# Odd tokens' rows by block transposes, their mean square by column sums, and three low parts by DMA, in a one-core decoder trunk

## The chip, the core and the metric

The kernel runs on one core of one Trainium2 chip. The metric is the device time of one execution in microseconds (us), the median of several runs. The engines are named as the profile names them: PE is TensorE's matrix multiplier (PEld its weight loads), DVE is VectorE, ACT is ScalarE, POOL is GpSimd, which here only issues accumulating DMAs, and SP is SyncE, which issues the other DMAs. Each of them runs its own instructions in order and waits on semaphores for the others.

## What is computed

One layer of a decoder trunk on x of 1024 tokens by 1024 channels, in fp32: a mixing block, then an MLP. The change lies where the first residual ends and the MLP begins:

```python
m = jax.nn.sigmoid(sa) * y_a + jax.nn.sigmoid(sb) * y_b
x = x + jnp.einsum("bsd,de->bse", m, w_o[l])          # called x1 here

h = rms_norm(x, g_mlp[l])                              # x / sqrt(mean(x*x) + EPS) * g
f = jnp.square(jax.nn.relu(jnp.einsum("bsd,df->bsf", h, w_1[l])))
x = x + jnp.einsum("bsf,fd->bsd", f, w_2[l])
return rms_norm(x, g_final)
```

## The kernel before

Activations lie with channels on the 128 partitions and tokens along the free axis. The tokens are held as even and odd ones: `x1[kk, o, c2]` is a tile of 128 x 1024 with o = 0 for even and o = 1 for odd tokens; its two halves are two blocks of 128 channels, kk and c2 say which. x1 thus has four tiles for each kind of token (x1000, x1001, x1100, x1101 and x1010, x1011, x1110, x1111 in the profile's full names, which the shown rows cut to `x`).

The three large products (w_a_out "a", w_o "o", w_1 "u") each run as seven block products of half size (p = 1 to 7, in the order 1, 2, 6, 7, 4, 5, 3) for four pairs of row blocks i. Every operand is split in a high part, rounded to the matmul's format, and a low part, the rest; a block product is 4 x 3 = 12 matmuls of 512 columns: high x high, high x low, low x high. The right operand's parts are `g{w}{p}h` and `g{w}{p}l` (halves 0 and 1 by c2), the left one's `o{i}_{p}` or `g{w}{i}_{p}` (both parts in one tile).

A low part is made in one of two ways. `low`: ACT copies the high part, DVE subtracts it from the source. `split_dma` (L61 to L67): ACT writes minus the rounded source (L65), POOL issues a DMA that adds the source to it (L66), ACT copies the high part (L67); DVE isn't used. Today the second operand of "u" (p = 2) and most left operands go the second way.

The stretch in question is written out by hand: `gseq` lists the block products in order, n counts them, and `GX[n]` names what else is recorded in step n; a small planner (`clk`, `at`, `dve`, `later`, `vector_work`, `flush`) decides where DVE's instructions stand among each other. Steps o0 = 28 to u0 = 56 are the products with w_o; from u0 the first eight products with w_1 follow (p = 1 for i = 0 to 3: banks gu0a to gu3a, then p = 2 on the same banks). Behind them the loop over `useq` continues with p = 6, 5, 7, 3, 4 for i = 0 and 1 (banks f0b, f1b, f0c, f1c, f0d, f1d, f0c, f1c, f0d, f1d), then the other row blocks.

For the even tokens (`x1_sq`, `x1_add`, `x1_turn`, `x1_cols`, `x1_root`, `x1_diag`, `x1_spread`, `x1_normed`): ACT squares the eight halves, DVE adds the squares to one tile, four matmuls with a column of ones sum it over the channels (`cs`, 128 tokens on partitions each), DVE and ACT form the root and its reciprocal (`stm`), diagonal matrices of it (`rdm`) times ones spread it over all partitions (`rbm`), and DVE normalises x1 in place. `x1_turn` transposes x1 in blocks of 32 x 32 on DVE (a row kk, th is one tile `x1r`) and SP writes them to DRAM; `x_block` reads them back in the second matrix stage (`d`), eight DMAs a block, as the residual's rows. The odd tokens have another way: `x1_rows` (step u0) transposes their x1 with 32 PE instructions into PSUM (`tr`), ACT squares and sums each row from there, DVE copies the rows out, SP writes them, and `x_block` reads a block with one DMA.

The left operands of "u" with p = 5, 6, 7, 3 for i = 0, 1 are sums of blocks of w_1: `up_lhs` makes s1, s2, s4, s3 (tiles `s`, five buffers in turn, so that the sixth, s4_1, takes s1_0's) on DVE and splits them by `split_dma` to o0_6, o1_6, o0_5, o1_5, o0_7 and so on.

Of the kernel before, what the change touches and what calls it, by code (L numbers as in the profile page):

```python
# [9 lines left out]
F32 = mybir.dt.float32  # L10
F32R = mybir.dt.float32r
I32 = mybir.dt.int32
AF = mybir.ActivationFunctionType
ALU = mybir.AluOpType

P = 128
S = 1024
# [13 lines left out]
def trunk_kernel(ctx: ExitStack, tc: tile.TileContext, x, xt_in, xt_eo, vecs, w_in, w_a_out, w_b_out,  # L31
# [1176 lines left out]
    def g_parts(w, p, c2):  # L1208
# [3 lines left out]
        if w == "u" and p == 2:  # L1212
            split_dma(src, h, l)
            at("A", 2.0)
            return
# [3 lines left out]
    def g_t(w, c2, *ns):  # L1219
# [4 lines left out]
        b11, b12, b21, b22 = (r[kk, o, c2] for kk in range(2) for o in range(2))  # L1224
# [41 lines left out]
    def g_mm(w, i, p):  # L1266
# [4 lines left out]
        for k in range(4):  # L1271
            h, l = (a[w, p, k // 2][:, HALVES[k % 2]] for a in (gh, gl))
# [97 lines left out]
    x1d = dp.tile([4, P, D], F32, name="x1d")  # L1370
    x1t = dp.tile([2, 2, P, S], F32, name="x1t")


    sqs = []

    def x1_sq(i, m_):
        s = EV(f"sq{i}{m_}")
        nc.scalar.activation(s, x1[i // 2, 0, i % 2][:, HALVES[m_]], AF.Square)
        sqs.append((at("A", 0.62, clk["V"]), s))

    def x1_add(n=1):
        for _ in range(n):
            ready, s = sqs.pop(1)
            later(ready, 0.63, tt, sqs[0][1], sqs[0][1], s, ALU.add)

    def x1_turn(kk):
        for th in range(2):
            r = T(f"x1r{kk}{th}")
            for c2 in range(2):
                src = x1[kk, 0, c2].rearrange("p (m h b j) -> p h m b j", m=2, h=2, j=32)[:, th]  # L1390
# [3 lines left out]
            nc.sync.dma_start(x1t[kk, th], r)  # L1394

    def x1_cols():

        sqs.append(bank("cs"))
        for n in range(4):
            nc.tensor.matmul(sqs[1][:, n:n + 1], sqs[0][1][:, n * P:(n + 1) * P], ones[:, 0:1],  # L1400
                             start=True, stop=True)
        at("P", 0.9)

    def x1_rows(*ts):
        for t in ts:
            o, n = divmod(t, 4)
            if n == 0:
                rst[o] = cp.tile([P, 6, 4], F32, tag="st6", name=f"stm{o}", bufs=2)
            rows = T(f"x1r{t}")
            for kk in range(2):  # L1410
                ps = bank(f"tr{t}{kk}")
                for c in range(4):
                    nc.tensor.transpose(ps[:, c * P:(c + 1) * P],
                                        x1[kk, o, c // 2][:, c % 2 * HS + n * P:c % 2 * HS + (n + 1) * P],
                                        ident)
                at("P", 0.45)
                if (t, kk) == (4, 0):
                    unread = T("sq")
                a = unread[:, HALVES[kk]]
                nc.scalar.activation(a, ps, AF.Square, accum_out=rst[o][:, kk, n:n + 1])  # L1420
                at("A", 0.63, clk["P"])

                def copy(rows, kk, ps, t):
                    nc.vector.tensor_copy(
                        rows[:, HALVES[kk]].rearrange("p (g c j) -> p c g j", g=4, c=4),
                        ps.rearrange("p (c g j) -> p c g j", g=4, c=4))
                    if kk:
                        nc.sync.dma_start(x1d[t - 4], rows)

                later(clk["P"], 0.63, copy, rows, kk, ps, t)  # L1430
            if t == 7:
                x1_root(1)
            if o:
                vector_work(clk["V"])

    def x1_root(o):

        if o == 0:
            rst[o] = cp.tile([P, 6, 4], F32, tag="st6", name=f"stm{o}", bufs=2)
        a, b, v, s = (rst[o][:, i, :] for i in range(4))  # L1440
        if o:
            tt(v, a, b, ALU.add)
# [666 lines left out]
```

## Time and profile before

| | |
|---|---|
| median of 3 runs | 1544.25 us (1544.06 to 1544.28) |
| the profiled execution | 1544.42 us |
| its span, first to last instruction | 1542.6 us |
| granted TensorE clock | 0.999 |
| instructions | 19197 |

The profile is of one execution. Its page gives the busy time of each engine and the chain of work that ended last; a timeline lists instructions in order of time, start and length in us, with neighbours of one kind merged (x32 is 32 of them, the length then from the first's start to the last's end), and in brackets the idle time before one and what ended it. Matmuls overlap: a single one is listed with 0.39 us, but starts follow each other every 0.23. In the rows of one line, a group has its count, then the shortest, median and longest duration in ns and the first and last start; a DMA's time to landing is counted from the start of its issue. A row of windows has the window, its length, and then each engine's busy time and instructions (PE, PEld, DVE, ACT, POOL), the clock, the DMA share and GB/s.

### The profile page before, as it was taken

The numbers are of one execution on the slowest core, as the hardware profiler recorded it, in microseconds if no ns is written. First come the engines' busy times: TensorE is split into PE (matmuls) and PEld (weight loads), VectorE is DVE, ScalarE is ACT, GpSimd is POOL, SyncE is SP. The second block draws the span as 40 slices with busy tenths as digits, with TensorE's granted clock in tenths as the row PEclk, the third lists the DMA queues.
The fourth block names the chain that finished last, engine by engine and source line by source line (L and its number), as shares of the span: only waits on it lengthen the run. The fifth ranks groups of instructions, "written<-read, shape, count | busy, mean of one in ns | idle before, by whom it ended". The sixth has DMA issues, their size and how long they took to land.

```text
span 1542.6 us, 19197 instructions
## 1 busy us (share of the span) xinstructions
PE 1533.0 (99%) x6782; PEld 1260.9 (82%) x6782; DVE 1222.4 (79%) x1648; ACT 903.7 (59%) x1261; POOL 184.4 (12%) x219
## 2 busy tenths in 40 slices
PE   9999999999999999999999999999999999999998
PEld 7888788888888888888888888888888888888886
DVE  6899999978999997478579889755555558888897
ACT  6648576567567667445275777554444475555553
POOL 0000000002222222000022332000000001111110
PEclk9999999999999999999999999999999999999999
DMA  8776978898997889953579897333333779998862
GB/s 347 195 192 159 251 189 218 220 273 212 254 253 196 194 194 240 316 174 111 181 204 297 200 219 180 137 123 112 112 114 112 240 217 231 223 224 220 209 130 110
DMA packets 132032, 307.82 MB, mean 200 GB/s; under 512 B 13488, under 2 KB 35504, under 8 KB 131936
## 3 DMA queue, kind: packets, MB, share of 16 engines
q1 hardware_dynamic: 101488, 230.60, 46.0%
q0 software_dynamic: 30304, 75.74, 26.9%
q8 instruction: 53, 0.87, 0.2%
q14 instruction: 43, 0.35, 0.1%
q10 hardware_dynamic: 144, 0.26, 0.0%
HBM read 147.69 MB, written 58.72 MB: 134 GB/s over the span
## 4 chain that ended last, share of the span: by engine, by line
PE 93%; DMA 2%; issue 2%; DVE 1%; ACT 0%; POOL 0%; SPq 0%; POOLq 0%; DVEq 0%
PE z L726 18%; PE d L1866 15%; PE yb L1097 8%; PE e L1993 3%; PE keep L1866 2%; PE z L258 1%; PE rg L534 1%; PE rg L536 1%; PE rg L535 1%; DMA x<-in_x_dram 1%; DMA zo<-zs 1%; DVE x L462 0%; DMA o<-s 0%; DMA xc<-in_xt_dram 0%; PE f1d L1552 0%
## 5 line engine op out<-in xcount | busy, mean ns | idle before, releaser
L726 PE MATMUL z<-xh,win_h 128*128 128x512 f32 x400 | 124.9, 390 | 0.0
L726 PE MATMUL z<-xl,win_h 128*128 128x512 f32 x400 | 124.5, 389 | 0.0
L1878 DVE TENSOR_TENSOR acc<-acc,d 128x1024 f32<-128x1024 f32 x72 | 87.8, 1219 | 33.3 <-PE d L1866 32.7
L726 PE MATMUL z<-xh,win_l 128*128 128x512 f32 x400 | 98.2, 391 | 0.0
L726 PEld LDWEIGHTS z<-xh,win_l 128*128 128x128 f32 x400 | 75.1, 188 | 16.9
L726 PEld LDWEIGHTS z<-xh,win_h 128*128 128x128 f32 x400 | 75.0, 188 | 16.7 <-ACT win_h L67 0.7
L637 DVE SCALAR_TENSOR_TENSOR y<-u,vec,y 128x511 f32<-128x511 f32 (+14 forms) x120 | 88.2, 735 | 0.0
L726 PEld LDWEIGHTS z<-xl,win_h 128*128 128x128 f32 x400 | 75.1, 188 | 15.8
L542 ACT ACTIVATE g<-rg,vec 96x1024 f32<-96x1024 f32 x32 | 35.6, 1112 | 85.0 <-issue 43.2
L637 DVE SCALAR_TENSOR_TENSOR yt<-u,vec,yt 128x511 f32<-128x511 f32 (+6 forms) x112 | 82.4, 736 | 0.0
L637 DVE SCALAR_TENSOR_TENSOR y<-yt,csum,y 128x511 f32<-128x511 f32 (+6 forms) x112 | 82.4, 736 | 0.0
L66 POOL DMA_DIRECT2D win_l<-win_raw x25 | 21.8, 871 | 324.6 <-ACT win_l L65 313.4
L1540 ACT ACTIVATE o<-s 128x512 fp32r<-128x512 f32 x56 | 33.7, 623 | 45.7 <-DVE s L1524 26.4
L66 POOL DMA_DIRECT2D zo<-zw x42 | 36.6, 872 | 130.4 <-ACT zo L65 113.5
L486 DVE SCALAR_TENSOR_TENSOR v<-xb,vec,v 128x1023 f32<-128x1023 f32 (+2 forms) x36 | 46.2, 1282 | 7.1 <-ACT v L477 6.3
L1097 PE MATMUL yb<-hgh,wb_h 128*128 128x512 f32 x168 | 51.7, 389 | 0.0
L1097 PE MATMUL yb<-hgl,wb_h 128*128 128x512 f32 x168 | 51.7, 389 | 0.0
L66 POOL DMA_DIRECT2D db_1l<-wr x7 | 6.1, 870 | 309.5 <-ACT db_1l L65 286.9
L1097 PE MATMUL yb<-hgh,wb_l 128*128 128x512 f32 x168 | 41.0, 389 | 0.0
L1063 DVE TENSOR_TENSOR o<-s,o 128x512 fp32r<-128x512 f32 x56 | 37.3, 683 | 1.4 <-ACT o L1540 1.4
L65 ACT ACTIVATE zo<-zw 128x512 fp32r<-128x512 f32 x42 | 26.2, 625 | 20.1 <-PE z10f L914 2.1
L1097 PEld LDWEIGHTS yb<-hgh,wb_h 128*128 128x128 f32 x168 | 31.5, 188 | 6.6
(1805 smaller groups left out, 4667.0 us busy)
## 6 DMA issues: line engine op xcount, KB each, us to landing
w_raw<-in_w_dram SPq DMA_DIRECT2D x34, 512.0 KB, 5.6
fr<-fd SPq DMA_DIRECT2D x32, 512.0 KB, 6.2
wr<-in_w_dram SPq DMA_DIRECT2D x32, 512.0 KB, 6.5
zw<-in_w_in_dram SPq DMA_DIRECT2D x28, 512.0 KB, 6.3
win_raw<-in_w_in_dram SPq DMA_DIRECT2D x25, 512.0 KB, 6.8
win_l<-win_raw POOLq DMA_DIRECT2D x25, 512.0 KB, 6.9
zo<-zw POOLq DMA_DIRECT2D x42, 256.0 KB, 5.7
gates<-zg SPq DMA_DIRECT2D x32, 256.0 KB, 3.8
```

Source lines behind the costliest of these rows:

```text
L65: nc.scalar.activation(l, src, AF.Copy, scale=-1.0)
L66: nc.gpsimd.dma_start(l, src, accum_op=ALU.add)
L486: nc.vector.scalar_tensor_tensor(v[:, d:S], a[:, 0:S - d], cbw_c[:, w * 12 + t:w * 12 + t + 1], v[:, d:S], ALU.mult, ALU.add)
L542: nc.scalar.activation(a, gps.pop((n, gi))[:HD, :], AF.Sigmoid, bias=(ba_c, bx_c)[gi][:, n:n + 1])
L637: nc.vector.scalar_tensor_tensor(o[:, k:], a[:, 0:HS - k], c, o[:, k:], ALU.mult, add)
L726: nc.tensor.matmul(zps[s][:, HALVES[hf]], w[:, k, :], xw[k][part][hf], start=n == 0, stop=n == 23)
L1063: tt(l, src, h.bitcast(F32), ALU.subtract)
L1097: nc.tensor.matmul(ps[hf], a, b[:, HALVES[hf]], start=n == 0, stop=n == len(todo) - 1)
L1540: nc.scalar.activation(o[:, 0], src, AF.Copy)
L1866: nc.tensor.matmul(o, a, b, start=n == 0 and (p != 1 or g == 0), stop=n == len(todo) - 1, skip_group_check=p == 1 and g > 0)
L1878: tt(acc[p, q2], acc[p, q2], ps, ALU.add)
L1993: nc.tensor.matmul(o, a, b, start=n == 0 and t not in LOADED, stop=n == len(todo) - 1, skip_group_check=t in LOADED)
```

## The change

The odd tokens take the even tokens' way. Their eight halves are squared on ACT between steps 23 and u0 (in another order, halves of p = 5 first), added on DVE, and summed over channels by four matmuls that stand in front of gu1a (`G_MID`); root and diagonals follow in step u0 + 1, and the spread in front of gu2a (before it stood in front of gu3a). `x1_turn` takes the token kind and a list of row halves: the odd tokens' first two tiles are transposed on DVE ahead of the last additions to x1 and the squares (step 27), the other two between the normalising of x1010, x1011 and that of x1110, x1111 (step u0 + 2). All of `x1_rows` is gone: 32 PE transposes, eight squares from PSUM, eight copies. `x_block` reads odd rows like even ones, with eight DMAs a block.

The low parts of the right operand p = 5 of "u" (gu5l0, gu5l1) and half of p = 1 (gu1l1) are made by `split_dma`. The left sums s1, s2 of w_1 and the operands made of them (o0_6 and others) are recorded one step later, and the parts of p = 5 and 6 in another order.

```diff
-        if w == "u" and p == 2:
+        if w == "u" and (p in (2, 5) or (p, c2) == (1, 1)):
             split_dma(src, h, l)
...
         for k in range(4):
+            if k == 0 and (w, p, i) in G_MID:
+                f, *a = G_MID[w, p, i]
+                f(*a)
...
-    x1d = dp.tile([4, P, D], F32, name="x1d")
-    x1t = dp.tile([2, 2, P, S], F32, name="x1t")
+    x1d = dp.tile([2, 2, 2, P, S], F32, name="x1d")
...
+    def x1_sq(o, i, m_):
+        n = len(sqt)
+        if o == 0 or 0 < n < 5:
+            s = EV(f"sq{o}{i}{m_}")
+        else:
+
+            if n in (0, 6):
+                x1_sq.t = T(f"sqs{n}")
+            s = x1_sq.t[:, HALVES[0 if n in (0, 6) else 1]]
+        if o:
+            sqt.append(s)
+        nc.scalar.activation(s, x1[i // 2, o, i % 2][:, HALVES[m_]], AF.Square)
+        sqs[o].append((at("A", 0.62, clk["V"]), s))
...
-    def x1_turn(kk):
-        for th in range(2):
-            r = T(f"x1r{kk}{th}")
+    def x1_turn(o, kk, *ths):
+        for th in ths:
+            r = T(f"x1r{o}{kk}{th}")
...
-    def x1_cols():
+    def x1_cols(o):
 
-        sqs.append(bank("cs"))
+        sqs[o].append(bank(f"cs{o}"))
         for n in range(4):
-            nc.tensor.matmul(sqs[1][:, n:n + 1], sqs[0][1][:, n * P:(n + 1) * P], ones[:, 0:1],
+            nc.tensor.matmul(sqs[o][1][:, n:n + 1], sqs[o][0][1][:, n * P:(n + 1) * P], ones[:, 0:1],
                              start=True, stop=True)
...
-    def x1_rows(*ts):
...
+    G_MID = {("u", 1, 1): (x1_cols, 1), ("u", 1, 2): (x1_spread, 1)}
...
-        23: ((x1_normed, 0, 0),), 24: ((g_parts, "u", 1, 0), (g_parts, "u", 1, 1)),
-        25: ((x1_normed, 1, 0),), 26: ((g_parts, "u", 2, 0),), 27: ((g_parts, "u", 2, 1),)}.items()})
+        23: ((x1_normed, 0, 0), (x1_sq, 1, 0, 1), (x1_sq, 1, 1, 1)), 24: ((g_parts, "u", 1, 0), (g_parts, "u", 1, 1), (x1_sq, 1, 2, 1)),
+        25: ((x1_normed, 1, 0), (x1_add, 1), (x1_sq, 1, 3, 1)),
+        26: ((g_parts, "u", 2, 0), (x1_add, 1, 2), (x1_sq, 1, 0, 0)),
+        27: ((g_parts, "u", 2, 1), (x1_add, 1), (x1_sq, 1, 1, 0), (x1_sq, 1, 2, 0), (x1_turn, 1, 0, 0, 1))}.items()})
     u0 = 2 * o0
     GX.update({u0 + n: v for n, v in {
-        0: ((g_lhs, "u", 1, 2), (up_lhs, 0, 6), (x1_rows, 4, 5, 6, 7)),
-        1: ((x1_diag, 1),), 2: ((x1_spread, 1), (up_lhs, 1, 6)),
-        3: ((x1_normed, 0, 1), (x1_normed, 1, 1), (g_t, "u", 0, 1), (g_t, "u", 1, 1)),
-        4: ((g_t, "u", 0, 2), (g_t, "u", 1, 2)), 5: ((g_parts, "u", 6, 0),),
-        6: ((g_parts, "u", 6, 1), (g_parts, "u", 5, 0), (up_lhs, 0, 5)),
-        7: ((g_parts, "u", 5, 1), (up_lhs, 1, 5), (g_t, "u", 0, 3), (g_t, "u", 1, 3))}.items()})
+        0: ((g_lhs, "u", 1, 2), (x1_add, 1, 2), (flush,), (x1_add, 1), (flush,)),
+        1: ((x1_root, 1), (x1_diag, 1), (up_lhs, 0, 6)),
+        2: ((x1_normed, 0, 1), (g_t, "u", 0, 1), (flush,), (up_lhs, 1, 6), (x1_turn, 1, 1, 0, 1),
+            (x1_normed, 1, 1)),
+        3: ((g_parts, "u", 5, 0), (g_t, "u", 0, 2), (flush,), (g_t, "u", 1, 1)),
+        4: ((g_t, "u", 1, 2), (g_parts, "u", 6, 0)),
+        5: ((g_parts, "u", 6, 1), (g_parts, "u", 5, 1)), 6: ((up_lhs, 0, 5),),
+        7: ((up_lhs, 1, 5), (g_t, "u", 0, 3), (g_t, "u", 1, 3))}.items()})
...
+            if n == u0:
+                x1_sq(1, 3, 0)
             g_get(n, g_mm)
...
     def x_block(b, q2):
         a = T(f"xb{b[0]}{b[1]}_{q2}")
-        if b[0]:
-            nc.sync.dma_start(a.rearrange("p (q c) -> p q c", q=2),
-                              x1d[2 * q2:2 * q2 + 2, :, b[1] * HS:(b[1] + 1) * HS].rearrange("q p c -> p q c"))
-            return a
-
-        src = x1t[b[1], q2].rearrange("(g i) (q b x) -> q b i g x", g=4, q=2, b=4)
+
+        src = x1d[b[0], b[1], q2].rearrange("(g i) (q b x) -> q b i g x", g=4, q=2, b=4)
```

72 lines of the change are left out of this document (19 added, 53 removed).

## The prediction

> **What bounds the kernel now.** I read the page first: busy time, then the chain of work that ended last.
>
> ```profile
> span 1542.6 us, 19197 instructions
> ...
> PE 1533.0 (99%) x6782; PEld 1260.9 (82%) x6782; DVE 1222.4 (79%) x1648; ACT 903.7 (59%) x1261; POOL 184.4 (12%) x219
> ...
> PE 93%; DMA 2%; issue 2%; DVE 1%; ACT 0%; POOL 0%; SPq 0%; POOLq 0%; DVEq 0%
> ```
>
> TensorE is busy 99% of the span and makes 93% of the chain. The change can gain only what it takes out of TensorE's own stream or out of its few waits there, and it loses whatever wait it puts in. Next I read TensorE's timeline around the odd tokens' rows (columns: start, length, engine, line, what, count).
>
> ```profile
> 897.40 0.95 PE L1400 MATMUL cs<-ones,sq 128*128 128x1 f32 x8
> 898.21 0.49 PE L1274 MATMUL go2e<-go5h,go 128*128 128x512 f32 x1
> ...
> 901.32 1.16 PE L1465 MATMUL rbm<-rdm,ones 128*128 128x128 f32 x8
> 902.24 0.48 PE L1274 MATMUL go3e<-go5h,go 128*128 128x512 f32 x1
> ...
> 918.66 3.65 PE L1413 MATMUL tr<-ident,x 128*128 128x128 f32 x32
> 922.07 0.48 PE L1274 MATMUL gu1a<-gu1h,gu 128*128 128x512 f32 x1
> ```
>
> ```profile
> 947.57 0.39 PE L1552 MATMUL f0c<-gu5h,o 128*128 128x512 f32 x1
> ...
> 953.01 0.39 PE L1552 MATMUL f0d<-gu7h,o 128*128 128x512 f32 x1
> ...
> 953.86 0.73 PE L1552 MATMUL f0d<-gu7h,o 128*128 128x512 f32 x2 [0.24 <-DMA o<-s]
> ...
> 959.20 0.39 PE L1552 MATMUL f0c<-gu3h,o 128*128 128x512 f32 x1
> ```
>
> Twelve matmuls make a product. From 947.57 to 953.01 two of them take 5.44 us without a wait, 2.72 each, 0.227 per matmul. The next two, to 959.20, take 6.19: there 0.75 us is lost today, as left low parts (o0_7, then o1_7) land late: the row at 953.86 names such a DMA as what ended its wait. From 959.20 on both kernels run the same instructions on TensorE, so how much earlier or later that matmul starts is the result.
>
> **Part 1, TensorE's own work.** Removed: 32 transposes, 918.66 to 922.07, 3.41 us. Added: four column sums, as the even tokens have them, 897.40 to 898.21, 0.81. What the step back to 512-wide matmuls costs stands behind either block and cancels. **Gain 2.60** if nothing waits.
>
> **Part 2, the wait that the column sums bring.** They stand behind gu0a, at 918.66, and need all eight odd squares added up. What VectorE does before that, from its rows:
>
> ```profile
> 887.32 1.48 DVE L462 TENSOR_TENSOR sq<-sq,sq 128x512 f32<-128x512 f32 x2
> ...
> 893.37 2.49 DVE L462 STREAM_TRANSPOSE x1r<-x 128x512 f32<-128x512 f32 x4
> 895.77 0.65 DVE L462 TENSOR_TENSOR x<-xe,go0e 128x512 f32<-128x512 f32 x1
> ...
> 899.34 0.13 DVE L1443 TENSOR_SCALAR stm<-cs 128x4 f32<-128x4 f32 x1
> ...
> 908.13 0.68 DVE L462 TENSOR_TENSOR x<-xe,go0e 128x512 f32<-128x512 f32 x1
> 908.73 2.72 DVE L462 SCALAR_TENSOR_TENSOR x<-x,vec,rbm 128x512 f32<-128x512 f32 x4
> 911.36 0.68 DVE L462 TENSOR_TENSOR x<-xe,go1e 128x512 f32<-128x512 f32 x1
> ...
> 936.40 2.36 DVE L462 TENSOR_TENSOR gt2u<-x,x 128x1024 f32<-128x1024 f32 x2
> 938.67 0.69 DVE L1528 TENSOR_TENSOR s<-w_raw,w_raw 128x512 f32<-128x512 f32 x1
> ...
> 946.54 0.68 DVE L1526 TENSOR_TENSOR s<-w_raw,s 128x512 f32<-128x512 f32 x1
> ...
> 953.00 1.22 DVE L1063 TENSOR_TENSOR gu7l<-x,gu7h 128x1024 fp32r<-128x1024 f32 x1
> ```
>
> Start to start an add takes 0.60 (908.13 to 908.73), one that needs the add before it about 0.71 (1.48 for two), four normalising steps 2.63 (908.73 to 911.36), four block transposes 2.40 (893.37 to 895.77), a 1024-wide subtraction 1.14 (936.40 to 938.67 is two). Normalising ends at 911.36 as before (gu1l1, gone to a DMA, may let it end 0.1 or 0.2 sooner). Then: a square add 0.60, an x1 add 0.60, two chained square adds 1.31, an x1 add 0.60: 914.5. Four block transposes, to 916.9; a square add 0.60; the last x1 add 0.60, to 918.1; three chained square adds 2.13: 920.2, with the head start 920.1. TensorE stands from 918.66 to 920.1, 1.45 us, and its weights then load uncovered: 0.92 for four small matmuls after a wait (901.32 to 902.24) against 0.81 in the stream (the sums at 897.40), 0.11 more. Behind the waiting sums stand gu1a and all that follows. Of the 2.60, **1.04 is left**. What is late is the last x1 add, as transposes run ahead of it. Bounds: no wait (2.60 kept) to 0.5 us more of it, should ScalarE's last square start one 512-wide step late.
>
> The four spread matmuls come one product earlier. Even tokens needed 1.98 from the variance (899.34) to the spread (901.32); here the sums end at 921.0 and their variance is read by 921.1, so 923.1, and gu1a (2.72) covers to 923.7. Without that cover TensorE would stand those 2 us.
>
> **Part 3, the fifth right operand.** Its parts cost VectorE 2 x 1.14 less and ScalarE 2 x 0.95 more, and ScalarE's order changes:
>
> ```profile
> 938.63 0.58 ACT L1331 ACTIVATE f<-gu1a 128x512 f32<-128x512 f32 x1
> ...
> 939.78 1.05 ACT L1216 ACTIVATE gu6h<-gt2u 128x1024 fp32r<-128x1024 f32 x1
> 940.73 1.04 ACT L1216 ACTIVATE gu5h<-x 128x1024 fp32r<-128x1024 f32 x1
> 941.68 0.62 ACT L65 ACTIVATE o<-s 128x512 fp32r<-128x512 f32 x1
> ```
>
> VectorE after the change: spread done 924.7, four normalising steps 2.63, one subtraction 1.14, two left sums 1.31 (the second needs the first), four transposes 2.40, four normalising steps 2.63, three 1024-wide and one 512-wide step 4.02: gt2u1 ends at about 939.0. Before it ended at 936.40 + 2.36 = 938.76. So TensorE's 1.04 is not passed on: the transposes that moved in here eat it. ScalarE then has gu6h1, gu5l1, gu5h1 (0.95 each, 939.78 to 940.73) and the two steps of f11_1 (1.15, 938.63 to 939.78) ahead of o0_5: 943.1 instead of 941.68. That copy feeds GpSimd's accumulating DMA, and f0c, 1.04 earlier at 946.53, wants its result with the third matmul, at 947.0.
>
> ```profile
> L66 POOL DMA_DIRECT2D o<-s x1: 872/872/872, 942.9 to 942.9; - x1
> ...
> DMA to landing us min/median/max: 3.3/3.3/3.3
> ```
>
> ```profile
> L66 POOL DMA_DIRECT2D gu2l<-x x1: 869/869/869, 911.5 to 911.5; - x1
> ...
> DMA to landing us min/median/max: 5.9/5.9/5.9
> ```
>
> ```profile
> L66 POOL DMA_DIRECT2D gu<-w_raw x1: 872/872/872, 913.0 to 913.0; - x1
> ...
> DMA to landing us min/median/max: 5.7/5.7/5.7
> ```
>
> GpSimd issues about 0.9 after the copy starts (less than the 1.2 from 941.68 to 942.9): 944.0. Alone it lands 3.3 later, 947.3. But gu5l1, 512 KB, is issued at 941.4 on the same queue (gu6h1 from 939.1, gu5l1's copy from 940.05 to 941.1, 0.3 more) and lands 5.9 later, 947.3; and a 256 KB transfer behind such a one landed 1.3 after it (911.5 + 5.9 = 917.4, 913.0 + 5.7 = 918.7), here 948.6. I take **948.2**, nearer to the pair, as this one follows 2.6 behind and not 1.5.
>
> [...]
>
> VectorE waits for that landing too: s4_1 takes the buffer of s1_0, which the DMA reads. From s4_1 to gu7l1 it needed 6.46 (946.54 to 953.00), and 1.22 for gu7l1 itself: landing + 7.7. TensorE wants gu7l1 at f0d's eighth matmul, 29 matmuls or 6.6 after the landing, and waits again for 1.1. Five more matmuls, 0.11 for the restart and f1d's 2.72 make 4.0. So f0c on gu3 starts at landing + 11.7 = 959.9, **0.7 later than 959.20**. The left low parts of this stage as a group:
>
> ```profile
> L66 POOL DMA_DIRECT2D o<-s x8: 869/869/880, 919.1 to 953.0; - x8
> ...
> DMA to landing us min/median/max: 3.3/6.5/7.8
> ```
>
> o1_7 is issued 2.4 behind o0_5's landing (two 512-wide steps, 1.4, and the issue) and wanted 9.4 behind it; with the worst 7.8 it would add 0.8, with the median nothing. I take 0.
>
> **Part 4, the rows by transposes.** VectorE loses eight PSUM copies and gains eight transposes. SyncE issues 28 more loads (8 for each of four blocks instead of one); the even tokens' show it:
>
> ```profile
> 1311.97 6.11 SPq L1890 DMA_DIRECT2D xb<-x1t  x8
> ...
> 1388.10 0.69 SPq L1883 DMA_DIRECT2D xb<-x1d  x1
> ```
>
> ```profile
> 1302.00:1340.00 38.00, 38.00 (x169) 31.40 (x168) 32.65 (x28) 20.83 (x22) 6.00 (x8) 1.00 0.91 222
> ```
>
> 5.4 us more of the queue, yet TensorE is full in the window that holds the eight (38.00 of 38.00): the loads' lead hides it. Cost 0; uncovered, 5.4 for each of the two blocks loaded inside the groups.
>
> [...]
>
> **Sum.** -2.60 + 1.56 (part 2) = -1.04 at f0c; the landing and gu7l1 turn that into +0.7: span 1543.3. The profiled execution took 1544.42, 1.8 more than its span and 0.17 over the median 1544.25: forecast 1544.95, say 1545.0.
>
> **Rivals.** First, the relief works: o0_5 lands alone, by 947.0; f0c doesn't wait, gu7l1 still does: 958.7, -0.5, 1543.8. For it: 3.3 above. Against: gu5l1 on the queue. Its far end, with no wait anywhere, is 2.60 + 0.75 = 3.35: 1540.9; against that stands part 2. Second, slower: GpSimd's queue backs up behind gu5l1, and o0_5 takes the group's median, 6.5. It lands at 950.5, f0c on gu3 starts at 962.2, +3.0, 1547.3, with o1_7's 0.8 1548.1. It turns to a loss once the landing is past 947.5; against it, w_1's next loads can't be issued before s3_1, which stands behind o0_5's landing. Third, the loads of part 4 aren't hidden: +5.4 and more; against it, the window.
>
> **Numbers.** Forecast 0.62 (its own range 1544.2 to 1546.2), relief 0.22, queue 0.13, loads 0.03. The range, 1543.4 to 1547.2, reaches into relief and queue and leaves out their far ends. A measurement can tell about 0.2% (3.1 us) from no change: faster by that, only the far end of the relief, 0.04; slower, half of the queue and the loads, 0.10; within, 0.86.
>
> **What would show it.** Column sums at about 920.1 with TensorE idle before, released by VectorE; gu1a at 921.0; f0c near 946.5 idle at its third matmul on o0_5's DMA; f0d idle on gu7l1; f0c on gu3 near 959.9; the groups' windows still full. Wrong if o0_5 lands before 947.0 or after 950, if the sums don't wait, or if TensorE idles behind the row loads.

## The result, and the profile after

Before the change: 1544.25 us (median of 7 runs, 1544.06 to 1544.76). After it: **1548.67 us** (median of 7, 1548.05 to 1551.11), a ratio of 1.0032 with a 95% interval of 1.0022 to 1.0042. The change made the kernel slower by 4.4 us. The forecast was 1545.0 with a range up to 1547.2, so the result lies beyond its upper end, near the far end (1548.1) of the rival in which GpSimd's queue backs up. The profiled execution after the change took 1548.05.

The page after the change, lines of its span, its busy times and its chain of work:

```profile
span 1546.3 us, 19183 instructions
...
PE 1532.5 (99%) x6758; PEld 1260.4 (82%) x6758; DVE 1223.6 (79%) x1651; ACT 907.0 (59%) x1256; POOL 187.5 (12%) x222
...
PE 96%; DVE 2%; DMA 1%; issue 1%; ACT 0%; SPq 0%; POOL 0%; DVEq 0%; POOLq 0%
```

TensorE's busy time fell from 1533.0 to 1532.5 and the span rose by 3.7. The 2.6 us less of transposes are hardly to be seen in it: part of what TensorE saved it spent on the same matmuls at a lower clock, as the next views show. Its waits after the change (what waited, for what; us in total, times, longest):

```profile
PE f0c L1529 <- DMA o<-s: 3.3, 1, 3.3
...
PE cs L1412 <- DVE sqs L462: 1.5, 1, 1.5
```

Before the change f0d's 0.2 was all that this view lists for this stage. TensorE's timeline (start, length, engine, line, what, count, the wait ahead of it):

```profile
919.79 1.05 PE L1412 MATMUL cs<-ones,sqs 128*128 128x1 f32 x8 [1.50 <-DVE sqs L462]
920.70 0.48 PE L1277 MATMUL gu1a<-gu1h,gu 128*128 128x512 f32 x1
...
923.55 1.05 PE L1442 MATMUL rbm<-rdm,ones 128*128 128x128 f32 x8
...
946.24 0.39 PE L1529 MATMUL f0c<-gu5h,o 128*128 128x512 f32 x1
946.46 0.39 PE L1529 MATMUL f0c<-gu5l,o 128*128 128x512 f32 x1
950.12 1.22 PE L1529 MATMUL f0c<-gu5h,o 128*128 128x512 f32 x2 [3.27 <-DMA o<-s]
...
962.04 0.39 PE L1529 MATMUL f0c<-gu3h,o 128*128 128x512 f32 x1
```

Three things stand here. The column sums wait 1.50. The spread follows gu1a without a wait. And f0c's third matmul, the first that reads the low part of o0_5, waits 3.27; the pair behind it then takes 1.22 us instead of 0.62. That is the clock. TensorE by windows of 1 us (window, us, busy and matmuls, granted clock, share of the DMA engines, GB/s):

```profile
949.00:950.00 1.00, 0.00 (x0) 0.80 1.03 244
950.00:951.00 1.00, 0.88 (x2) 0.50 1.10 252
951.00:952.00 1.00, 1.00 (x4) 0.50 0.80 145
952.00:953.00 1.00, 1.00 (x4) 0.50 0.63 86
953.00:954.00 1.00, 1.00 (x6) 1.00 0.85 307
```

While TensorE waits, its granted clock falls to half; it stays there until 953 although matmuls are running again. f0c's last ten matmuls take 3.74 (950.12 to f1c's start at 953.86) instead of 10 x 0.227 and 0.1 for the restart, 2.37: 1.4 us.

All executions start this stage at a slightly different time, so stages are compared from the start of gu0a to the start of f0c on gu3, called **the stage** below: 915.93 to 959.20 before, 43.27 us; 915.41 to 962.04 after, 46.63. The difference of the spans, 3.6 (3.7 from the rounded ones), is +3.36 in the stage, -0.52 ahead of gu0a, and about +0.8 behind f0c on gu3. This last piece lies behind TensorE's last matmul. The last copy of the output on ScalarE's queue, before (first fence) and after (second):

```profile
L2021 ACTq DMA_DIRECT2D out_dram<-out x1: 400/400/400, 1538.9 to 1538.9; - x1
...
DMA to landing us min/median/max: 2.8/2.8/2.8
```

```profile
L2002 ACTq DMA_DIRECT2D out_dram<-out x1: 393/393/393, 1541.7 to 1541.7; - x1
...
DMA to landing us min/median/max: 3.4/3.4/3.4
```

It lands 0.6 later after its issue, and the span ends some 0.3 later behind that.

### The profile page after: what moved, and what is told of

It reads as the page before. It is cut to its first block, busy times and chain, and to the rows that moved or that the text cites. A ratio compares the mean times of both kernels' runs of the same rounds, so it can differ in the third digit from the quotient of the medians.

```text
span 1546.3 us, 19183 instructions
## 1 busy us (share of the span) xinstructions
PE 1532.5 (99%) x6758; PEld 1260.4 (82%) x6758; DVE 1223.6 (79%) x1651; ACT 907.0 (59%) x1256; POOL 187.5 (12%) x222
## 4 chain that ended last, share of the span: by engine, by line
PE 96%; DVE 2%; DMA 1%; issue 1%; ACT 0%; SPq 0%; POOL 0%; DVEq 0%; POOLq 0%
PE z L726 18%; PE d L1851 15%; PE yb L1097 8%; PE e L1974 3%; PE keep L1851 2%; PE z L258 2%; PE rg L534 1%; PE rg L536 1%; PE rg L535 1%; DVE x L462 1%; DVE x1r L462 1%; PE f0c L1529 0%; DMA o<-s 0%; DMA xc<-in_xt_dram 0%; PE f1c L1529 0%
## 5 line engine op out<-in xcount | busy, mean ns | idle before, releaser
L1097 PEld LDWEIGHTS yb<-hgl,wb_h 128*128 128x128 f32 x168 | 31.5, 188 | 6.6
```

The source lines that it names most:

```text
L1097: nc.tensor.matmul(ps[hf], a, b[:, HALVES[hf]], start=n == 0, stop=n == len(todo) - 1)
```

## Experiments

Each variant was timed against the kernel before in runs of its own batch (medians of 1544.14 to 1544.43); the ratios are to those. The variants start from the changed kernel unless something else is said. "Profiled stage" is the length of the stage as defined above in the variant's own profile, which is of one run: in third_left_first its lowest (1545.51), in loads_alone and third_left_first_early7 their highest (1546.16 and 1546.76).

| variant | median, us | ratio, 95% interval | profiled stage, us |
|---|---|---|---|
| before | 1544.25 | 1 | 43.27 |
| after | 1548.67 | 1.0032 [1.0022, 1.0042] | 46.63 |
| gu5_vector | 1547.78 | 1.0024 [1.0015, 1.0033] | 45.42 |
| gu5_one | 1545.38 | 1.0009 [1.0000, 1.0018] | 45.02 |
| left5_first | 1548.18 | 1.0026 [1.0016, 1.0036] | 45.08 |
| sums_in_place | 1550.00 | 1.0043 [1.0031, 1.0056] | 50.12 |
| fill | 1548.45 | 1.0026 [1.0016, 1.0036] | 46.78 |
| turn_late | 1549.45 | 1.0033 [1.0020, 1.0046] | 47.03 |
| turn_late_gu5_one | 1546.47 | 1.0014 [1.0005, 1.0023] | 43.78 |
| turn_late_gu5_one_in_place | 1546.07 | 1.0010 [1.0001, 1.0019] | 44.11 |
| loads_alone (from before) | 1544.24 | 1.0001 [0.9993, 1.0010] | 43.27 |
| third_left_first | 1546.95 | 1.0017 [1.0008, 1.0026] | 43.30 |
| swap | 1547.76 | 1.0022 [1.0013, 1.0031] | 45.32 |
| swap_turn_late | 1547.07 | 1.0019 [1.0010, 1.0028] | 44.25 |
| third_left_first_early7 | 1545.20 | 1.0005 [0.9996, 1.0014] | 42.69 |
| before_early7 (from before) | 1543.44 | 0.9993 [0.9984, 1.0002] | 42.55 |

**What made o0_5 late: the fifth right operand's low part ahead of it.** Three variants take it out of the way in three manners.

```diff
@@ gu5_vector @@
-        if w == "u" and (p in (2, 5) or (p, c2) == (1, 1)):
+        if w == "u" and (p == 2 or (p, c2) == (1, 1)):
@@ gu5_one @@
+        if w == "u" and (p == 2 or (p, c2) in ((1, 1), (5, 0))):
@@ left5_first @@
-        5: ((g_parts, "u", 6, 1), (g_parts, "u", 5, 1)), 6: ((up_lhs, 0, 5),),
+        5: ((g_parts, "u", 6, 1), (up_lhs, 0, 5)), 6: ((g_parts, "u", 5, 1),),
```

> The changed kernel with the fifth right operand's low parts (gu5l0, gu5l1) back on VectorE. In the changed kernel o0_5's accumulating DMA was issued at 943.8 and landed 6.3 us later, at 950.1, and f0c stood 3.3 us for it. From the landing to the start of f0c on gu3 it took 11.9 us. Theory 'queue': gu5l1's 512 KB, issued at 941.2 ahead of it on GpSimd's queue, is what made it late. Then o0_5, issued at about 944.0, lands after 3.3 to 4.4 us (947.3 to 948.4), f0c waits at most 1.2, and f0c on gu3 starts 1.7 to 2.8 us earlier than in the changed kernel: 1545.2 to 1546.4 for a run like the profiled one of 1548.05. VectorE has two more subtractions of 1.14 ahead of gu6l1, which may cost f0b about 0.6 of that. Rival 'traffic': all transfers share the 16 DMA engines, and the spills of f to memory (fd<-f, 256 KB each, issued at 943 and 945) hold o0_5 up by themselves: it takes 5.4 as o1_5's did, lands at 949.4, and at most 0.7 us comes back.

> The changed kernel with only the second half of the fifth right operand (gu5l1) back on VectorE; gu5l0 stays a DMA. ScalarE has one copy of 0.95 us less ahead of o0_5, so its DMA is issued at about 942.9 instead of 943.8, and the transfer of gu5l0 (landed at 940.6) is out of its way. Theory 'queue': it lands after 3.3 to 4.4 us, at 946.2 to 947.3; f0c waits 0.6 us at most, and f0c on gu3 starts at 958.2 to 959.2 instead of 962.0: 2.8 to 3.8 us faster than the changed kernel, 1544.2 to 1545.3. Rival 'traffic': it takes 5.4 us, lands at 948.3, f0c waits 1.6: 1.9 us faster, 1546.2. If neither gu5l1 nor the copy matters (a third way: o0_5 is late because of something earlier), the time stays at 1548.

> The changed kernel with o0_5's copies and DMA put ahead of gu5l1's on ScalarE and GpSimd; nothing else differs. o0_5 is issued at about 940.8 and lands before 946, so f0c's third matmul no longer waits. gu5l1 is issued at about 943.4 instead of 941.2 and is wanted by f0c's eighth matmul at 947.8. Theory 'queue': with nothing ahead of it, it lands 5.2 us later, as it did, at 948.6; f0c waits 0.8 us there instead of 3.3 and f0c on gu3 starts 9.4 us later, at 958.0: 4.0 us faster than the changed kernel. Rival 'traffic': it shares the engines with o0_5 and two spills of f and takes 6.8 as gu5l0 did, lands at 950.2, f0c on gu3 at 959.6: 2.4 us faster, and the wait has only moved from o0_5 to gu5l1.

The issue of o0_5's DMA and its time to landing, in the changed kernel and in the three variants in this order (each fence is the view of that one instruction):

```profile
L66 POOL DMA_DIRECT2D o<-s x1: 872/872/872, 943.8 to 943.8; - x1
...
DMA to landing us min/median/max: 6.3/6.3/6.3
```

```profile
L66 POOL DMA_DIRECT2D o<-s x1: 872/872/872, 944.3 to 944.3; - x1
...
DMA to landing us min/median/max: 4.3/4.3/4.3
```

```profile
L66 POOL DMA_DIRECT2D o<-s x1: 869/869/869, 944.4 to 944.4; - x1
...
DMA to landing us min/median/max: 3.7/3.7/3.7
```

```profile
L66 POOL DMA_DIRECT2D o<-s x1: 872/872/872, 942.0 to 942.0; - x1
...
DMA to landing us min/median/max: 3.3/3.3/3.3
```

The four DMAs move the same 256 KB. With gu5l1's 512 KB 2.6 us ahead of it, it takes 6.3; without that 4.3 or 3.7, with the same spills of f beside it; with gu5l1 behind it instead of ahead 3.3, as in the kernel before. So gu5l1 ahead of it is what makes it late, as theory "queue" has it, and "traffic", the spills alone (5.4 without gu5l1), falls. That it is the place on GpSimd's queue is not shown: the spill of f that SyncE issues 0.8 ahead of o0_5 is slowed too, and takes 5.3 in the changed kernel

```profile
L1336 SPq DMA_DIRECT2D fd<-f x1: 319/319/319, 943.0 to 943.0; - x1
...
DMA to landing us min/median/max: 5.3/5.3/5.3
```

but 3.9 in gu5_vector and 2.5 in gu5_one, which have no gu5l1 there. The share of the 16 DMA engines reads 0.87 to 1.07 in windows of 1 us from 944 to 950 in the changed kernel; from 942 to 951 it is 0.98, which the queues' shares add up to (72.7%, 24.7% and 0.7%).

The time came back only in part. left5_first was forecast 4.0 faster than the changed kernel, and its median is 0.5 lower. In it the wait moved to the transfer that now stands second, and further to the next:

```profile
PE f0d L1529 <- DMA o<-s: 1.6, 1, 1.6
PE cs L1412 <- DVE sqs L462: 1.5, 1, 1.5
PE f0c L1529 <- DMA gu5l<-x: 0.9, 1, 0.9
```

gu5l1's wait of 0.88 was forecast (0.8); o0_7's of 1.55 was not. In gu5_vector f0b and f1b took 0.6 us more, as forecast for the two subtractions, and o0_5, gu7l1 and o1_7 were waited for one after the other, 0.8, 0.9 and 0.5. o0_5's DMA took 2.0 less and landed 1.8 sooner counted from gu0a; 1.2 of it is left in the stage, and 1547.26, its profiled execution, is above the forecast (1545.2 to 1546.4). gu5_one is the best of the three, though its median, 1545.38, is just above its forecast (1544.2 to 1545.3); o0_5's issue came 1.5 later than forecast (944.4, not 942.9), and for its 45.02 the clock behind the column sums has to be known, the next point.

**The half clock after a wait.** TensorE by windows of 1 us behind the column sums of gu5_one, which waited 1.50 as in the changed kernel:

```profile
920.00:921.00 1.00, 1.00 (x10) 1.00 1.09 240
921.00:922.00 1.00, 1.00 (x4) 0.60 1.06 250
922.00:923.00 1.00, 1.00 (x4) 0.50 1.00 283
923.00:924.00 1.00, 1.00 (x4) 0.50 1.03 305
924.00:925.00 1.00, 1.00 (x4) 0.70 1.11 215
```

Four windows lose 0.4 + 0.5 + 0.5 + 0.3 = 1.7 us. Less that, its stage would be 43.3, that of the kernel before; no run of it without the drop was profiled. The same wait of 1.5 at the column sums stands in six profiles. In three (after, gu5_vector, left5_first) the clock stayed whole, in gu5_one and swap it was halved for about 3.4 us, in sums_in_place for about twice that, 3.4 us lost. The wait of 3.2 to 3.3 for o0_5 stands in three profiles (after, sums_in_place, turn_late) and was followed by the half clock in all. In the changed kernel the clock fell 0.5 us ahead of the restart, in the two others 1.0 and 1.5 us behind it. Of the other waits, 1.55 in left5_first and 1.64 in swap_turn_late brought no half clock, nor did any shorter one in this stage (the longest is 1.46, in swap_turn_late). But the profile of loads_alone (a variant of the kernel before, below) has one of 1.62 near the start of the program, with full matmuls behind it, and the granted clock falls there as well, from 9.2 to 12.6, 1.7 us lost:

```profile
8.37 0.50 PE L258 MATMUL z<-xh,w_h 128*128 128x512 f32 x1 [1.62 <-ACT xh L227]
```

```profile
10.00:11.00 1.00, 1.00 (x3) 0.50 1.00 406
11.00:12.00 1.00, 1.00 (x4) 0.50 1.04 418
```

So the column sums' tiny passes are not needed for it. What decides whether the clock falls behind a wait of this length, no run shows.

To take the clock away without the waits, matmuls whose results are overwritten were put into both waits, and to take away what hangs on o0_5's landing on VectorE, s3_0 and s3_1 were written over raw weights:

```diff
@@ fill, in g_mm and in up_mm @@
+                if i == 1:
+                    for _ in range(6):
+                        nc.tensor.matmul(gb[w, i, b], o[:, 0, 0, :], gh[w, p, 0][:, HALVES[0]],
+                                         start=True, stop=True)
...
+        if (i, p) == (0, 5):
+            for _ in range(14):
+                nc.tensor.matmul(ps, o[:, 0, 0, :], gh["u", p, 0][:, HALVES[0]],
+                                 start=True, stop=True)
@@ sums_in_place, in up_lhs @@
-            tt(S(3), blk(0, 0), blk(1, 0), ALU.subtract)
+            sv[i, 3] = blk(1, 0) if i < 2 else S(3)
+            tt(sv[i, 3], blk(0, 0), blk(1, 0), ALU.subtract)
```

> The changed kernel with matmuls whose results are thrown away put into TensorE's two waits: 6 of 128x512 (1.4 us) ahead of the column sums and 14 (3.2 us) ahead of f0c, each into a bank that the next product overwrites. They wait for nothing that the product itself doesn't wait for, so what TensorE waits for still comes at the same time. Theory 'clock': after a wait TensorE is granted half its clock for about 3.4 us or twice that, in the changed kernel after f0c's wait in the profile (950.1 to 953.3) and after the column sums in some runs (it was seen there in two of four variants). Full TensorE keeps the whole clock: granted 0.999 in every run, the runs lie within 1 us of each other instead of 3, and the median comes down by about 1 us from 1548.7 to about 1547.7, as what comes out of f0c then waits for gu7l1. Rival 'clock is only a symptom': the spread of the runs comes from landing times, and 20 more matmuls bring nothing or cost: 1548.7 or more, with the same spread.

> The changed kernel with the two sums s3_0 and s3_1 written over a block of the raw weights that only they still need, so that s4_1 finds a free buffer and no longer waits on VectorE for o0_5's landing; o0_5 itself is as late as before. Theory 'clock and wait': what costs is f0c's own wait of 3.3 us and the half clock after it (10 matmuls in 3.7 us instead of 2.3). Then gu7l1 and o1_7 come some 6 us earlier and nobody needs them earlier: f0c on gu3 stays within 0.3 us of 962.0, time 1548. Rival 'buffer': the stall of 6.2 us on VectorE is what holds TensorE back through gu7l1 and o1_7: 1 us or more comes back.

In fill TensorE's granted clock is 1.00 in every window of the stage, and its 8 runs lie between 1547.64 and 1549.05, where those of the changed kernel reach 1551.11: the upper runs are gone, as they would be if they were the clock's. The lower ones did not come down, and the median, 1548.45, missed the forecast of 1547.7. What waits instead is the wait the prediction had in this place:

```profile
PE f0d L1537 <- DVE gu7l L1063: 0.9, 1, 0.9
PE cs L1416 <- DVE sqs L462: 0.2, 1, 0.2
```

In the changed kernel gu7l1's lateness is hidden behind the half clock; with the full clock it is seen. So the half clock behind o0_5's wait costs 1.4 us on TensorE and next to nothing of the time, while that behind the column sums costs 1.7 or 3.4 in the profiles that have it.

sums_in_place freed VectorE of its wait (6.2 us in the changed kernel) and brought nothing, as "clock and wait" forecast: of its stage of 50.12, 3.4 is the half clock behind the column sums, and the 46.7 that are left are the changed kernel's 46.63. Its median, 1550.0, is above the forecast 1548, probably for the same reason: four of its five runs have a mean clock of 0.995 or 0.997.

**The column sums' wait.** The first four transposes were put behind the chain to 1/rms, alone and with gu5_one, and with both edits above:

```diff
-        27: ((g_parts, "u", 2, 1), (x1_add, 1), (x1_sq, 1, 1, 0), (x1_sq, 1, 2, 0), (x1_turn, 1, 0, 0, 1))}.items()})
+        27: ((g_parts, "u", 2, 1), (x1_add, 1), (x1_sq, 1, 1, 0), (x1_sq, 1, 2, 0))}.items()})
...
-        1: ((x1_root, 1), (x1_diag, 1), (up_lhs, 0, 6)),
+        1: ((x1_root, 1), (x1_diag, 1), (x1_turn, 1, 0, 0, 1), (up_lhs, 0, 6)),
```

> The changed kernel with the first four of the odd tokens' block transposes (x1r100, x1r101) behind the chain to 1/rms instead of ahead of the last x1 addition; nothing else differs. The four take 2.4 us on VectorE ahead of the column sums, more than the 1.5 that TensorE waits there. Theory: the column sums then follow gu0a without a wait, gu1a starts 1.5 us earlier, and normalising, ScalarE and o0_5's issue come earlier by the same, so that f0c's wait of 3.3 us and the half clock behind it stay: 1.5 us faster than the changed kernel where the clock behind the sums is whole, and 1.6 or 3.2 more in the runs where it was halved: median 1546.5. Rival: the moved transposes hold up normalising instead (they stand ahead of it on VectorE), gt2u1 and f0b come late, and nothing or 1 us is gained.

> Both: the four transposes behind the chain to 1/rms, and the second half of the fifth right operand back on VectorE. From the parts: the column sums don't wait, o0_5 is issued at about 941.4 and lands after 3.7 to 4.3 us, so f0c waits 0.5 at most; s4_1 still waits for its landing on VectorE, so gu7l1 is ready 7.7 later and f0d waits 1.0 to 1.6 for it. From gu0a's start to f0c on gu3: 41.5 to 42.2 us instead of 46.6 (before the change: 43.3). Time 1542.5 to 1543.2, faster than before the change by 1 to 2 us. Rival: loads and low parts collide in the shorter stretch (o1_7 took 7.2 us in the variant with one half), and it is no better than before, 1544 or more.

> As the one before, and s3_0 and s3_1 written over raw weights, so that s4_1 doesn't wait for o0_5's landing. If gu7l1 behind that buffer is what is left, f0d doesn't wait either: 40.2 to 40.7 us from gu0a to f0c on gu3, time 1541.2 to 1541.8. Rival: o0_7 and o1_7 then are issued earlier, but land after 8 to 9 us, as in the variant with that edit alone, and f1d waits for o1_7 about 1 us: no gain over the variant without it.

The waits of turn_late:

```profile
PE f0c L1529 <- DMA o<-s: 3.2, 1, 3.2
...
PE gu3a L1277 <- DMA gu<-w_raw: 1.1, 1, 1.1
PE cs L1412 <- DVE sqs L462: 0.3, 1, 0.3
```

The column sums wait 0.26 instead of 1.50 and gu1a starts 1.2 us earlier against gu0a. Yet f0b starts 25.55 after gu0a against 25.39 in the changed kernel (940.80 - 915.41): the whole gain is given back at gu3a, which waits for a low part that hangs on VectorE's sums through ScalarE's order (third_left_first, below, changes that order and has no wait there). And o0_5 lands no earlier, so its wait is as long as before. The forecast of 1546.5 missed; 1549.45 was measured, no better than the changed kernel. The rival was right: normalising starts 9.8 us after gu0a (925.30 - 915.53) instead of 9.2 (924.64 - 915.41), as the moved transposes stand ahead of it now. With gu5_one the forecasts (1542.5 to 1543.2, 1541.2 to 1541.8) missed in the same way: 1546.47 and 1546.07, with waits for gu3_2, gu7l1, or o0_7 and o1_7 in the place of those removed.

**The loads of the rows, alone.** From the kernel before:

```diff
-            nc.sync.dma_start(a.rearrange("p (q c) -> p q c", q=2),
-                              x1d[2 * q2:2 * q2 + 2, :, b[1] * HS:(b[1] + 1) * HS].rearrange("q p c -> p q c"))
+            for q in range(2):
+                for n in range(4):
+                    nc.sync.dma_start(a[32 * n:32 * n + 32, HALVES[q]],
+                                      x1d[2 * q2 + q, 32 * n:32 * n + 32, b[1] * HS:(b[1] + 1) * HS])
```

> The kernel before the change with one thing changed: each of the four odd blocks of residual rows is loaded by eight DMAs of 32 partitions instead of by one, 28 issues more on SyncE, as after the change. Forecast by the prediction: nothing, as the loads lead by much; within 0.2 us of the kernel before. Rival: the eight issues push the next loads back, 5.4 us for each of two blocks inside the groups: 1549 or more. Also open: in the changed kernel and in all eight variants of it the last two DMAs to the output landed 3.4 and 3.0 us after their issue, in the kernel before 2.8 and 2.6, and from f0c on gu3 to the end it took 584.2 to 584.5 us instead of 583.4. If the issues on SyncE's queue are the cause, this kernel shows 3.4 and 3.0 too and is 0.9 us slower; if not, it shows 2.8 and 2.6.

1544.24, ratio 1.0001, stage 43.27: 28 issues more cost nothing, as forecast. (The profiled run is 1546.16 mostly because of the wait near the start and the half clock that were shown above: gu0a starts at 917.42, 1.5 later than before.) The last copy to the output lands after 2.9, so the issues are not what made it 3.4 in the changed kernel. It was 3.4 in ten of its variants and 2.9 in third_left_first and third_left_first_early7, which have the change's row writes and loads too. What sets it stays open.

**Does the relief of TensorE ever show?** Four variants tried to bring the operands forward as well, and a fifth makes the last of these moves in the kernel before. A call of `up_lhs` with p = 0 computes the two sums of that i alone. The swaps have gu5_vector's edit and swap_turn_late that of turn_late too; both, third_left_first_early7 and before_early7 have that of sums_in_place. Not shown of the swaps: the parts of p = 5 and o1_5 are recorded in steps u0 + 2 and u0 + 3, and f0c and f1c are added up when f0b and f1b are done.

```diff
@@ third_left_first, from turn_late_gu5_one @@
-        2: ((x1_normed, 0, 1), (g_t, "u", 0, 1), (flush,), (up_lhs, 1, 6), (x1_turn, 1, 1, 0, 1),
+        2: ((x1_normed, 0, 1), (g_t, "u", 0, 1), (flush,), (up_lhs, 1, 0), (x1_turn, 1, 1, 0, 1),
...
-        3: ((g_parts, "u", 5, 0), (g_t, "u", 0, 2), (flush,), (g_t, "u", 1, 1)),
+        3: ((up_lhs, 1, 6), (g_parts, "u", 5, 0), (g_t, "u", 0, 2), (flush,), (g_t, "u", 1, 1)),
...
-    UX = {0: ((g_parts, "u", 7, 0), (g_t, "u", 0, 4)), 1: ((g_parts, "u", 7, 1), (g_t, "u", 1, 4)),
-          2: ((g_parts, "u", 3, 0),), 3: ((g_parts, "u", 3, 1),), 4: ((g_parts, "u", 4, 0),),
+    UX = {0: ((g_parts, "u", 7, 0),), 1: ((g_parts, "u", 7, 1),),
+          2: ((g_parts, "u", 3, 0), (g_t, "u", 0, 4)), 3: ((g_parts, "u", 3, 1), (g_t, "u", 1, 4)), 4: ((g_parts, "u", 4, 0),),
@@ swap, swap_turn_late @@
-        1: ((x1_root, 1), (x1_diag, 1), (up_lhs, 0, 6)),
+        1: ((x1_root, 1), (x1_diag, 1), (up_lhs, 0, 6), (up_lhs, 0, 5)),
...
-    useq = [(i, p) for p in ORDER[1:4] + (3, 4) for i in range(2)]
+    useq = [(i, p) for p in (5, 6, 7, 3, 4) for i in range(2)]
@@ third_left_first_early7, from third_left_first @@
-        5: ((g_parts, "u", 6, 1), (g_parts, "u", 5, 1)), 6: ((up_lhs, 0, 5),),
-        7: ((up_lhs, 1, 5), (g_t, "u", 0, 3), (g_t, "u", 1, 3))}.items()})
+        5: ((g_parts, "u", 6, 1), (g_parts, "u", 5, 1)), 6: ((up_lhs, 0, 5), (up_lhs, 0, 7)),
+        7: ((up_lhs, 1, 5), (up_lhs, 1, 7), (g_t, "u", 0, 3), (g_t, "u", 1, 3))}.items()})
...
-    ready = 4
+    ready = 6
```

> The variant with late transposes and one half of the fifth right operand on VectorE, and two more things in another order: gu3_2's copies and DMA stand ahead of o1_6's on ScalarE (there o1_6's copy waits for VectorE's s2_1, and TensorE waited 1.1 us for gu3_2's low part in both variants with late transposes), and the two subtractions x1100 and x1101 come behind gu7l1 on VectorE (TensorE waited 0.9 for gu7l1). If each wait was what it looked like, f0b starts 24.4 us after gu0a instead of 25.5, and f0c on gu3 41.6 to 42.0 after it instead of 43.8: 1544.1 to 1544.5 instead of 1546.5. Rival: behind gu3_2's wait stands VectorE, whose stream from the column sums to gu6l1 has no gap: gu6l1 then is not ready before 26.8 after gu0a, f0b waits about 0.9 for it, and f0c on gu3 starts 42.6 to 42.9 after gu0a: 1545.2.

> The changed kernel with the order of two products changed for the first two output tiles: f0c and f1c (right operand 5) before f0b and f1b (right operand 6), both halves of operand 5 from VectorE, o0_5 and o1_5 copied beside o0_6 and o1_6, and s3_0, s3_1 written over raw weights. Operand 5 is ready before operand 6, which hangs on the end of the normalising chain, so VectorE gains 5.4 us for gu6l1, and no low part of the right side stands ahead of o0_5 on GpSimd's queue. Theory 'operands late': f0c starts 25.4 us after gu0a as f0b did and nothing waits before o0_7; f0c on gu3 starts 41.7 to 43.0 us after gu0a instead of 46.6: 1543.4 to 1544.7, and up to 3 more in runs in which the clock is halved behind the column sums. Rival: other waits take their place (gu5l1, whose subtraction now stands amid the normalising chain), and it is 1546 or more.

> As the one before, with the first four block transposes behind the chain to 1/rms. TensorE doesn't wait at the column sums, so the clock has no reason to fall there: the runs lie within 1.5 us of each other. VectorE has the 2.4 us of transposes ahead of the first normalising steps now, of which about 0.6 is seen at gu5l1. Theory: f0c starts 24.2 to 25.0 us after gu0a, f0c on gu3 41.0 to 42.0: 1542.7 to 1543.7, faster than before the change by 0.5 to 1.5 us. Rival: gu3_2 and o0_7 land late as before in this stage, and it stays at 1544 to 1546.

> As third_left_first, and the copies and DMAs of o0_7 and o1_7 stand right behind those of o0_5 and o1_5 on ScalarE instead of behind the spills of f, s3_0 and s3_1 are written over raw weights, and by that the sums s4_0, s3_0 come behind gu6l1 on VectorE. Theory 'late operands hid the relief': gu6l1 is ready 1.2 us earlier and f0b doesn't wait, o0_7 and o1_7 land by 950, f0d and f1d don't wait; f0b starts 24.2 us after gu0a and f0c on gu3 40.5 to 41.3: 1541.3 to 1543.0, and the relief of 2.6 us is there at last. Rival: o0_5 and o1_5 share GpSimd's queue with o0_7 now and land late instead, f0c waits 1 to 3 us, 1544 or more.

> The kernel before the change with the same move of o0_7 and o1_7 and the same two sums over raw weights, and nothing of the change. Theory: only the 0.75 us that f0d and f1d lost to o0_7 and o1_7 comes back: f0c on gu3 42.5 us after gu0a instead of 43.3, time 1543.4 to 1543.6. If the move alone brings as much as in the other variant (2 us or more), the change's relief of TensorE is worth nothing here even then; if it brings nothing or costs, other operands are late too.

third_left_first gets TensorE to f0b 24.15 us after gu0a, 2.05 earlier than before the change: the relief is real. Then it waits 0.61 for gu6l1 (the rival's 0.9 was near) and 0.91 for o0_7, and its stage is 43.30. A further 1.2 is lost right behind the stage (f3b starts 25.68 after f0c on gu3, before the change 24.48), and its median, 1546.95, is above its forecast (1544.1 to 1544.5) and its rival's 1545.2. The two swaps had other waits in their place: 1.24 for o0_7; 1.64 for gu5l1 and 1.46 for o0_7. Both forecasts (below 1544.7 and 1543.7) missed; 1.2 of that lies behind the stage, where both wait 0.9 for `fb` at the first matmuls of `keep`. third_left_first_early7 brings o0_7 forward, and the wait shows up at the next transfer in the queue:

```profile
PE f1c L1532 <- DMA o<-s: 0.9, 1, 0.9
...
PE f2c L1532 <- ACT fb L1580: 0.5, 1, 0.5
...
PE f0b L1532 <- DVE gu6l L1063: 0.2, 1, 0.2
PE f0c L1532 <- DMA o<-s: 0.2, 1, 0.2
```

Its stage is 42.69, its median 1545.2; the forecast of 1541.3 to 1543.0 missed. That it is slower than the kernel before with a shorter stage comes from behind the stage: from f0c on gu3 to the end it took 585.3 us (1545.0 - 959.74) against 583.4. Of the 1.9, 1.4 is lost right behind the stage, where f2c waits for `fb` and f0d for gu4l (f3b starts 25.87 after f0c on gu3 instead of 24.48): probably a price of the order in which x1100 and x1101, on which gu4l hangs, were put. before_early7, the same move without the change, has none of these waits; the row below is from TensorE's timeline in it, and its stage is 42.55 (958.53 - 915.98):

```profile
958.53 0.39 PE L1553 MATMUL f0c<-gu3h,o 128*128 128x512 f32 x1
```

Its median, 1543.44, is where it was forecast (1543.4 to 1543.6), 0.9 below the kernel before of the same batch (1544.36). It has the lowest median of all kernels here, though the interval of the ratio still reaches 1.0002. With the transposes still on TensorE it is as far at the end of the stage as the best variant without them, and when f3b starts it is 1.4 us ahead of it, counted from gu0a.

## Why the prediction was wrong

**Right.** The column sums wait 1.50 (forecast 1.45) and gu1a starts 5.29 after gu0a (forecast 5.07, 921.0 - 915.93); the spread is covered. gt2u1 ends at 938.85 (forecast 939.0), o0_5's copy starts at 942.89 (943.1) and its DMA is issued at 943.80 (944.0); counted from gu0a, which starts 0.52 earlier than before, these three are 0.3 to 0.4 late. VectorE's chain behind the landing is right to a few hundredths: its timeline has gu7l1 done 7.73 us after f0c's release at 950.12 (forecast 7.7),

```profile
956.63 1.22 DVE L1063 TENSOR_TENSOR gu7l<-x,gu7h 128x1024 fp32r<-128x1024 f32 x1
```

and f0c on gu3 starts 11.9 after the landing (forecast 11.7). That this sum fits is in part luck: the wait of 1.1 that was forecast at f0d for gu7l1 did not come, because f0c's half clock, which the sum doesn't have, had taken 1.4 before it. The loads are hidden: f0c on gu3 is 2.84 later than before, and so, within 0.01, are the first group of the down stage and the last stage.

**Wrong: the landing of o0_5.** The step that failed is "I take 948.2, nearer to the pair, as this one follows 2.6 behind and not 1.5." The transfer ahead was named rightly, and the term was mis-sized. Measured was 950.1. gu5l1 itself was quick (5.2, forecast 5.9, landed at 946.4), but o0_5 came 3.7 behind it, not the 1.3 of the pair. What the two stretches have in flight differs. The queues by what they carried (packets, MB, share of the 16 engines), for the pair before the change, 910 to 919, where only GpSimd's queue (q0) has a row beside the one named instruction,

```profile
q0 software_dynamic: 690, 1.72, 104.8%
```

and after the change, 942 to 951, with SyncE's issues on q1:

```profile
q0 software_dynamic: 490, 1.17, 72.7%
q1 hardware_dynamic: 423, 0.77, 24.7%
```

The prediction took the pair's 1.3 over into a stretch in which SyncE also spills f, and put those spills at nothing. Behind gu5l1's landing three transfers of 256 KB land in 3.9 us: the spill issued at 943.0 at 948.3, o0_5 at 950.1, the spill issued at 945.2 at 950.3; at the pair's 1.3 each, three make 3.9. This fits, but no run takes the spills away, so it is not shown as the cause.

The row that would have served was the median of the group, 6.5, which stood in the prediction as the rival's price: 6.3 was measured, and the rival's f0c on gu3, 962.2, was measured at 962.04, the half clock included. In the order of the sum this is +2.4 us at the landing, counted from gu0a, of the 2.7 that the stage is longer than forecast (46.63 against 959.9 - 915.93 = 43.97). The rival had 0.13; with a row for each side at hand, one pair and a group of eight, its chance should have been nearer to that of the forecast, and the range should have reached its far end.

**Not in the prediction: what a wait does to the clock.** In the profile before TensorE never waited longer than 0.8 us after its first matmul (at 1.60), and its granted clock reads 1.00 in every window of 1 us up to its last one. In three profiles of variants the column sums' wait of 1.5 is followed by 1.7 us (gu5_one, swap) or 3.4 us (sums_in_place) lost to the half clock. That is probably where the upper runs come from: the four lower ones have a mean clock of 0.998 and lie within 0.6 us, the three upper ones have 0.996 or 0.997. That the clock behind the column sums is halved in these three runs is inferred from fill and from the profiles of the variants; the one profile of the changed kernel is of a run without it. Not every spread is of this kind: the kernel before reached 1546.68 in the batches of the variants at a mean clock of 0.999 or 1.0.

**Not in the prediction: the end.** About 0.8 behind f0c on gu3, mostly the last copy to the output. It isn't the issues of the row loads (loads_alone); its cause wasn't found.

**The far end of the relief, 1540.9, was reached by no variant.** The prediction set it against part 2 alone. The runs point to a wider reason: TensorE's operands in this stage come from VectorE's and ScalarE's streams and from the low parts on GpSimd's queue, and the change leaves those about as long as they were (over the whole span VectorE is busy for 1222.4 us before and 1223.6 after, ScalarE for 903.7 and 907.0, GpSimd for 184.4 and 187.5). VectorE's eight copies of 683 ns became eight transposes of 678 ns, three subtractions of it became three DMAs, and seven additions of squares came in. In third_left_first and third_left_first_early7 TensorE arrives 2 us earlier at f0b (24.15 and 24.13 after gu0a against 942.13 - 915.93 = 26.20), and both then spend it on waits for gu6l1, o0_5, o1_5 or o0_7 and, behind the stage, for gu4l and `fb`.

## What to carry to other kernels

Work taken from the busiest engine paid here only as far as the operands behind it came earlier too: before counting the gain, list for each of its next products when each part is ready today, and take as the gain the smallest slack among them. A transfer that was put ahead of another was paid here by the one behind it (o0_5 landed 6.3 us after its issue behind gu5l1, and 3.3 ahead of it in left5_first), so its price was what the next small transfer lacked in slack, and not its own lateness. A time from landing to landing did not carry over here from one stretch to another (1.3 us in the pair, 3.7 where SyncE's queue moved 0.77 MB beside it): compare what each queue moves in both before taking one. A new wait of 1.5 us or more on TensorE should be priced with a chance of the half clock, once or twice 1.7 us (it came behind four of nine waits of 1.5 to 1.64 between matmuls here and behind all three of 3.2 or more), and with a spread of the runs.

## What was not expected of the hardware

A wait of TensorE of 1.5 us ahead of the column sums was followed by the half clock in three of six profiles, and in one of them it lasted about 6.8 us: granted clock 0.50 from 921 to 927, gu1a's matmuls among them. With the same waits filled with matmuls that do nothing it stayed at 1.00, the highest run was 2 us lower (1549.05 against 1551.11), and the median was no higher. And the last copy of the same 256 KB to the output took 2.8 to 2.9 us in some kernels and 3.4 in others, in profile after profile of one kind or the other, though no edit touches the code around it.
